# First x ahead of the vectors, first weights on ScalarE's queue, and of them only the first channel tile's columns at the beginning

## The chip, the core and the metric

The kernel runs on one core of one Trainium2 chip. The metric is the device time of one execution in microseconds (us), and lower is better. A profile of one execution was taken by the hardware profiler; its times, and all the rows below, are in us from the start of the span that the profile covers unless ns is written.

## What is computed

The reference is one layer of an encoder that works on 1024 frames of 1024 channels in float32. Cut to what matters here:

```python
h = rms_norm(x, norm1_g)
u = h @ w_in                                   # 1024 x 3072
u_conv, q, k, v, g = jnp.split(u, split_at, axis=-1)
a_out = conv_group(u_conv, ...)                # a * sigmoid(gate), causal conv of 31 taps, LayerNorm, silu
b_out = retention_group(q, k, v, g, ...)       # rotary, chunked retention, per-head RMSNorm, silu gate
x = x + concatenate([a_out, b_out]) @ w_out
h = rms_norm(x, norm2_g)
x = x + square(relu(h @ w_ff1)) @ w_ff2
return rms_norm(x, final_g)
```

The change touches only the beginning: the loads for `x`, for the first columns of `w_in` (those of `u_conv`), and the matmuls that use them.

## The kernel before

Every float32 operand of a large matmul is split in two parts, high and low: ScalarE writes a rounded copy (`split_row`, L116, for weights; `split_col`, L252, for columns of x, with the norm's gain as scale) and VectorE writes the rest (L117, L253). `mm3` (L149 to L151) multiplies high by high, high by low and low by high into one PSUM accumulator.

The program begins with `u_conv`. The x columns come as eight tiles `xc[i][h]` (i: a quarter of the 1024 channels, two rows of 128 each; h: a half of the frames), the weights as four tiles `raws[i]` of 128 x 2 x 512 (512 KB). A `raws[i]` holds four blocks of 128 columns: value and gate columns of channel tile j = 0, then those of channel tile j = 1. The loop at L326 goes through i; for each it splits `xc[i][0]`, `raws[i]` and `xc[i][1]` and issues the matmuls of channel tile 0 (`glu_proj(w, 0, ...)`), which use only the first 256 columns. The second 256 columns are used for the first time at L342, in `glu_proj(w, 1, ...)`.

Behind the loop come, in the code's order: the load of `dec`, then `stats(t)` for eight token blocks (load of 128 rows of x as `xt`, the sum of squares by ScalarE at L165, two small GpSimd operations), then `n2d` (L339), which writes 1024 single floats from `vec` to memory, 4 KB in all. Then TensorE does channel tile 1 for the first half of the frames (L342), and `pb` (L352): eight small matmuls of the matrix of ones with `diag` tiles that GpSimd builds from the norms (L351). ScalarE copies each half of `pb` out as `row` (L354). Then `trg` is loaded, `glu_gate(first)` runs, and `chunk_w(0)` loads and splits the next weights (`load_raw`, L112, then `split_row` on whole tiles); the remaining matmuls of channel tile 1 follow (second half of the frames).

What sets the order: TensorE, ScalarE and VectorE follow the code inside the `manual_schedule` block at L319; everywhere else, and for all transfers that SyncE issues, a scheduler arranges the instructions by their expected times, subject to the dependences. Each engine then carries out its own list strictly in that order, and one that waits holds up what stands behind it. All loads here are issued by SyncE (SPq in the rows). The weights' raw tiles come from the pool `rawp`, which has two buffers:

```python
rawp = pool("rawp", 2)
cp = pool("cp", 7)
```

so `raws[2]` takes the buffer of one of the first two tiles once that one has been split for the last time, and the transfer waits for this. The accumulators lie in two pools of four PSUM banks, `ps` and `pr`; `pb`'s two tiles and the accumulators of channel tile 1 take banks of `pr`, so the matmuls of channel tile 1's second half need the banks that `row` frees. Before the first real matmul TensorE does eleven matmuls of ones (L323), two passes each.

Of the kernel before, what the change touches and what calls it, by code (L numbers as in the profile page):

```python
# [8 lines left out]
F32 = mybir.dt.float32  # L9
F32R = mybir.dt.float32r  # L10
BF16 = mybir.dt.bfloat16
AF = mybir.ActivationFunctionType
ALU = mybir.AluOpType
PSUM = bass.MemoryType.PSUM

P = 128
D = 1024
S = 1024
CW = 512
# [6 lines left out]
ND = D // P  # L26
# [15 lines left out]
def hybrid_layer_kernel(  # L42
# [14 lines left out]
    nc = tc.nc  # L57
# [4 lines left out]
    rawp = pool("rawp", 2)  # L62
# [29 lines left out]
    cols = {}  # L92
# [19 lines left out]
        nc.sync.dma_start(raw, src)  # L112
        return raw

    def split_row(raw, w, i):
        nc.scalar.activation(w[:, 0, i], raw[:, i], AF.Copy)  # L116
        nc.vector.tensor_tensor(w[:, 1, i], raw[:, i], w[:, 0, i].bitcast(F32), ALU.subtract)  # L117

    def split(raw, scales):

        w = wp.tile([P, 2] + list(raw.shape[1:]), F32R, tag="w", name="w")
        for i in range(raw.shape[1]) if scales else [slice(None)]:
            if scales is None:
                split_row(raw, w, i)
            else:
                nc.scalar.activation(w[:, 0, i], raw[:, i], AF.Copy, scale=scales[i])
                nc.vector.scalar_tensor_tensor(
                    w[:, 1, i], raw[:, i], scales[i], w[:, 0, i].bitcast(F32), ALU.mult, ALU.subtract
                )
        return w  # L130
# [79 lines left out]
    def chunk_w(c):  # L210
        return [load_split(w_in[c, i], None) for i in range(ND // 2)]
# [32 lines left out]
    def split_cols(raw, dp, h):  # L244

        for i in range(2):
            split_col(raw, dp, h, i)

    def split_col(raw, dp, h, i):
        d = 2 * dp + i  # L250
        hi, lo = hT.half(d, 0, h), hT.half(d, 1, h)
        nc.scalar.activation(hi, raw[:, i], AF.Copy, scale=col("n1", d))  # L252
        nc.vector.scalar_tensor_tensor(lo, raw[:, i], col("n1", d), hi.bitcast(F32), ALU.mult, ALU.subtract)  # L253
# [16 lines left out]
    def glu_accs(j):  # L270
        return [[bank(j) for _ in range(2)] for _ in range(2)]

    def glu_proj(w, j, accs, d, h):

        for q in range(2):
            lo = (2 * j + q) * P
            mm3(
                accs[q][h],
                w[d // 2][:, 0, d % 2, lo : lo + P],
                w[d // 2][:, 1, d % 2, lo : lo + P],  # L280
                hT.half(d, 0, h),
                hT.half(d, 1, h),
                d == 0,
                d == ND - 1,
            )
# [18 lines left out]
    for h in range(2):  # L304
        hT.new(h)
    xc = [[cp.tile([P, 2, HALF], F32, tag="c", name="xcol") for _ in range(2)] for _ in range(ND // 2)]
    nc.sync.dma_start(vec, vecs)
    raws = [rawp.tile([P, 2, CW], F32, tag="raw", name="raw") for _ in range(ND // 2)]
    for i in range(2):
        nc.sync.dma_start(xc[0][0][:, i], x_cols[0, 0][:, i])  # L310
        nc.sync.dma_start(raws[0][:, i], w_in[1, 0][:, i])
    nc.sync.dma_start(xc[0][1], x_cols[0, 1])
    for i in range(1, ND // 2):
        nc.sync.dma_start(xc[i][0], x_cols[i, 0])
        nc.sync.dma_start(raws[i], w_in[1, i])
        nc.sync.dma_start(xc[i][1], x_cols[i, 1])
    w = []
    accs = glu_accs(0)
    with tc.manual_schedule(engines=ordered):  # L319

        idle = pr.tile([P, 4, P], F32, tag="r", name="idle")
        for i in range(WARM):
            nc.tensor.matmul(idle[:, i % 4], lhsT=ones, rhs=ones, start=True, stop=True)  # L323
        warm = tiny.tile([P, 1], F32, tag="ss1", name="warm")
        nc.scalar.activation(warm, mhalf[:, 0:1], AF.Square)
        for i in range(ND // 2):  # L326
            w.append(wp.tile([P, 2, 2, CW], F32R, tag="w", name="w"))
            for k in range(2):
                split_col(xc[i][0], i, 0, k)
                split_row(raws[i], w[i], k)  # L330
            split_cols(xc[i][1], i, 1)
            for h in range(2):
                for d in (2 * i, 2 * i + 1):
                    glu_proj(w, 0, accs, d, h)
# [39 lines left out]
    for g in range(NG):  # L374
        if g == NG - 1:
            w = chunk_w(2)
# [39 lines left out]
    w = wk  # L416
# [191 lines left out]
    i = 0  # L608
# [468 lines left out]
```

## Time and profile before

| what | value |
|---|---|
| median of 3 runs | 1037.97 us (1037.92 to 1038.72) |
| the profiled execution's own time | 1039.08 us |
| its span (first to last instruction) | 1037.1 us |
| mean granted TensorE clock in the span | 0.998 |
| TensorE busy | 1022.5 us, 99% |
| VectorE busy | 801.1 us, 77% |
| ScalarE busy | 380.9 us, 37% |
| GpSimd busy | 137.3 us, 13% |

The span is shorter than the execution's own time by 2.0 us, which lie before the first and behind the last instruction. A row of the timeline gives the start, the duration, the engine, the line in the code, what is written and read, how many instructions are merged in it, and in brackets how long the engine stood idle before and what released it. The rows of SPq are issues of transfers; the bytes land later.

### The profile page before, as it was taken

Reading aid. Unit: us, or ns where it says so; the run is one execution under the profiler, and the core shown is the slowest. Engines: PE = TensorE matmul, PEld = TensorE weight load, DVE = VectorE, ACT = ScalarE, POOL = GpSimd, SP = SyncE. Lnnn points to the kernel's source line nnn. Section 1 sums busy time; section 2 is a strip of 40 time slices with the busy share of each in tenths; the row PEclk is TensorE's granted clock in tenths of the full one; section 3 lists DMA queues with packets and bytes.
Section 4 is the critical chain, followed back from the end, with each engine's and each line's share of the span. In section 5 each row is a group of like instructions: output and inputs, shape, how many; then the busy total and the mean of one; then the engine's idle time right before and its main releaser. Section 6 shows DMA issues by size and latency. Waiting matters only on the chain.

```text
span 1037.1 us, 12617 instructions
## 1 busy us (share of the span) xinstructions
PE 1022.5 (99%) x4726; PEld 848.1 (82%) x4726; DVE 801.1 (77%) x981; ACT 380.9 (37%) x596; POOL 137.3 (13%) x253
## 2 busy tenths in 40 slices
PE   9999999999999999999999999999999999999997
PEld 7788888898888888878888888887888888888885
DVE  6297787998797659987777767766998778778765
ACT  7521121044531465543232333233443433433442
POOL 0410110012200233112121211211100000000013
PEclk9999999999999999999999999999999999999999
DMA  9722021102042047665363443548565355255214
GB/s 356 150 77 73 8 82 41 41 21 83 1 153 92 21 161 265 207 218 190 136 206 129 162 163 122 182 164 303 177 209 194 102 183 168 96 188 177 89 54 162
DMA packets 52876, 145.38 MB, mean 140 GB/s; under 512 B 6864, under 2 KB 16208, under 8 KB 52816
## 3 DMA queue, kind: packets, MB, share of 16 engines
q1 hardware_dynamic: 38000, 107.35, 31.5%
q0 software_dynamic: 10592, 35.14, 8.7%
q10 hardware_dynamic: 4224, 2.10, 0.7%
q8 instruction: 37, 0.61, 0.2%
q14 instruction: 23, 0.19, 0.1%
HBM read 103.14 MB, written 41.42 MB: 139 GB/s over the span
## 4 chain that ended last, share of the span: by engine, by line
PE 53%; DVE 3%; DMA 2%; issue 1%; ACT 0%; SPq 0%; POOLq 0%; POOL 0%; ACTq 0%; DVEq 0%
PE acc L149 9%; PE acc L150 9%; PE acc L151 9%; PE pa L151 5%; PE pa L149 5%; PE pa L150 5%; PE pb L151 4%; PE pb L150 4%; PE pb L149 4%; DMA w2raw<-in_w_dram 2%; DVE w L203 1%; DVE blk L949 0%; DVE hid L758 0%; ACT w L200 0%; DVE w1l L203 0%
## 5 line engine op out<-in xcount | busy, mean ns | idle before, releaser
L149 PE MATMUL acc<-w 128*128 128x512 f32 x448 | 174.7, 390 | 1.1 <-DVE hid L758 0.8
L151 PE MATMUL acc<-w 128*128 128x512 f32 x448 | 174.3, 389 | 0.0
L150 PE MATMUL acc<-w 128*128 128x512 f32 x448 | 174.3, 389 | 0.0
L395 DVE SCALAR_TENSOR_TENSOR y<-glu,vec,y 128x1024 f32<-128x1024 f32 x120 | 153.7, 1289 | 2.0
L149 PEld LDWEIGHTS acc<-w 128*128 128x128 f32 x448 | 84.1, 188 | 20.0 <-issue 1.4
L149 PE MATMUL acc<-w,cols 128*128 128x512 f32 x256 | 100.1, 391 | 0.0
L150 PE MATMUL acc<-w,cols 128*128 128x512 f32 x256 | 99.8, 390 | 0.0
L151 PE MATMUL acc<-w,cols 128*128 128x512 f32 x256 | 99.8, 390 | 0.0
L151 PEld LDWEIGHTS acc<-w 128*128 128x128 f32 x448 | 84.1, 188 | 17.5
L150 PEld LDWEIGHTS acc<-w 128*128 128x128 f32 x448 | 84.1, 188 | 17.2
L200 ACT ACTIVATE w<-xr 128x1024 fp32r<-128x1024 f32 x56 | 59.2, 1058 | 98.8 <-PE acc L151 44.4
L203 DVE TENSOR_TENSOR w<-xr,w 128x1024 fp32r<-128x1024 f32 x56 | 68.3, 1220 | 28.2 <-ACT w L200 27.8
L949 DVE TENSOR_TENSOR blk<-acc,blk 128x512 f32<-128x512 f32 (+1 forms) x113 | 72.8, 680 | 17.0 <-PE acc L151 17.0
L149 PE MATMUL pa<-h,w1h 128*128 128x512 f32 x192 | 74.8, 393 | 0.5 <-ACT w1h L200 0.5
L151 PE MATMUL pa<-h,w1l 128*128 128x512 f32 x192 | 75.0, 392 | 0.1
L149 PE MATMUL pb<-h,w1h 128*128 128x512 f32 x192 | 74.8, 389 | 0.0
L151 PE MATMUL pb<-h,w1l 128*128 128x512 f32 x192 | 74.7, 389 | 0.0
L150 PE MATMUL pb<-h,w1h 128*128 128x512 f32 x192 | 74.7, 389 | 0.0
L203 DVE TENSOR_TENSOR w1l<-t,w1h 128x1024 fp32r<-128x1024 f32 x32 | 39.1, 1223 | 43.4 <-PE pb L150 40.1
L116 ACT ACTIVATE w<-raw 128x1024 fp32r<-128x1024 f32 (+1 forms) x32 | 30.5, 954 | 87.8 <-PE acc L151 70.3
L151 PEld LDWEIGHTS acc<-w,cols 128*128 128x128 f32 x256 | 48.1, 188 | 10.0
L149 PEld LDWEIGHTS acc<-w,cols 128*128 128x128 f32 x256 | 48.1, 188 | 9.8
(194 smaller groups left out, 2003.8 us busy)
## 6 DMA issues: line engine op xcount, KB each, us to landing
w1raw<-in_w_dram SPq DMA_DIRECT2D x32, 512.0 KB, 4.7
w2raw<-in_w_dram SPq DMA_DIRECT2D x32, 512.0 KB, 4.5
raw<-in_w_in_dram SPq DMA_DIRECT2D x23, 512.0 KB, 3.3
xt<-in_x_dram SPq DMA_DIRECT2D x8, 512.0 KB, 7.9
raw<-in_w_out_dram SPq DMA_DIRECT2D x8, 512.0 KB, 3.2
xr<-in_x_dram SPq DMA_DIRECT2D x16, 256.0 KB, 3.0
kept<-blk POOLq DMA_DIRECT2D x8, 512.0 KB, 3.3
blk<-kept SPq DMA_DIRECT2D x8, 512.0 KB, 4.7
```

The source lines that it names most:

```text
L116: nc.scalar.activation(w[:, 0, i], raw[:, i], AF.Copy)
L149: nc.tensor.matmul(acc, lhsT=lh, rhs=rh, start=first, stop=False, **kw)
L150: nc.tensor.matmul(acc, lhsT=lh, rhs=rl, start=False, stop=False, **kw)
L151: pe_log.append(nc.tensor.matmul(acc, lhsT=ll, rhs=rh, start=False, stop=last, **kw))
L200: act = nc.scalar.activation(hi, src, AF.Copy)
L203: nc.vector.tensor_tensor(lo, src, hi.bitcast(F32), ALU.subtract)
L395: nc.vector.scalar_tensor_tensor(y, glu[c][:, k : k + S], tap(k), y, ALU.mult, ALU.add)
L949: return nc.vector.tensor_tensor(t, acc[lane][r][:, lo:hi], t, ALU.add)
```

## The change

The load of the first half of `xc[0][0]` goes in front of that of the vectors `vec`. The first row of `raws[0]` is issued by ScalarE, as its first instruction, the second row by SyncE; both bring only the first 256 columns. The other 256 columns of both rows (`then`) are loaded by one transfer that stands in the code behind those of i = 2, and are split behind the loop's last splits.

```diff
-    def split_row(raw, w, i):
-        nc.scalar.activation(w[:, 0, i], raw[:, i], AF.Copy)
-        nc.vector.tensor_tensor(w[:, 1, i], raw[:, i], w[:, 0, i].bitcast(F32), ALU.subtract)
+    def split_row(raw, w, i, cols=slice(None)):
+        nc.scalar.activation(w[:, 0, i, cols], raw[:, i, cols], AF.Copy)
+        nc.vector.tensor_tensor(w[:, 1, i, cols], raw[:, i, cols], w[:, 0, i, cols].bitcast(F32), ALU.subtract)
...
+    raws = [rawp.tile([P, 2, CW], F32, tag="raw", name="raw") for _ in range(ND // 2)]
+    now, then = slice(0, 2 * P), slice(2 * P, CW)
+    nc.scalar.dma_start(raws[0][:, 0, now], w_in[1, 0][:, 0, now])
+    nc.sync.dma_start(xc[0][0][:, 0], x_cols[0, 0][:, 0])
     nc.sync.dma_start(vec, vecs)
-    raws = [rawp.tile([P, 2, CW], F32, tag="raw", name="raw") for _ in range(ND // 2)]
-    for i in range(2):
-        nc.sync.dma_start(xc[0][0][:, i], x_cols[0, 0][:, i])
-        nc.sync.dma_start(raws[0][:, i], w_in[1, 0][:, i])
+    nc.sync.dma_start(raws[0][:, 1, now], w_in[1, 0][:, 1, now])
+    nc.sync.dma_start(xc[0][0][:, 1], x_cols[0, 0][:, 1])
     nc.sync.dma_start(xc[0][1], x_cols[0, 1])
     for i in range(1, ND // 2):
         nc.sync.dma_start(xc[i][0], x_cols[i, 0])
         nc.sync.dma_start(raws[i], w_in[1, i])
         nc.sync.dma_start(xc[i][1], x_cols[i, 1])
+        if i == 2:
+            nc.sync.dma_start(raws[0][:, :, then], w_in[1, 0][:, :, then])
...
-                split_row(raws[i], w[i], k)
+                split_row(raws[i], w[i], k, now if i == 0 else slice(None))
             split_cols(xc[i][1], i, 1)
+            if i == ND // 2 - 1:
+                split_row(raws[0], w[0], slice(None), then)
```

SyncE's list, from the first transfer of i = 1 on. The number behind a name is that of the tile: before, `raws[0]` to `raws[3]` are raw_126 to raw_129, now they are raw_125 to raw_128; xcol_117 to xcol_124 are `xc[0][0]` to `xc[3][1]`. Before:

```order
L314 DMA xcol_119<-in_x_cols_dram 128x1024
L315 DMA raw_127<-in_w_in_dram 128x1024
L316 DMA xcol_120<-in_x_cols_dram 128x1024
L314 DMA xcol_121<-in_x_cols_dram 128x1024
L315 DMA raw_128<-in_w_in_dram 128x1024
L316 DMA xcol_122<-in_x_cols_dram 128x1024
L314 DMA xcol_123<-in_x_cols_dram 128x1024
L315 DMA raw_129<-in_w_in_dram 128x1024
L316 DMA xcol_124<-in_x_cols_dram 128x1024
L335 DMA dec_100<-in_decay_dram 128x576
L259 DMA xt_314<-in_x_dram 128x1024
```

There each `raws[i]` stood between the two x tiles of its i, and `raws[3]` ahead of `dec`. SyncE's list in the same place now:

```order
L316 DMA xcol_119<-in_x_cols_dram 128x1024
L317 DMA raw_126<-in_w_in_dram 128x1024
L318 DMA xcol_120<-in_x_cols_dram 128x1024
L316 DMA xcol_121<-in_x_cols_dram 128x1024
L318 DMA xcol_122<-in_x_cols_dram 128x1024
L317 DMA raw_127<-in_w_in_dram 128x1024
L320 DMA raw_125<-in_w_in_dram 128x2x256
L316 DMA xcol_123<-in_x_cols_dram 128x1024
L318 DMA xcol_124<-in_x_cols_dram 128x1024
L341 DMA dec_100<-in_decay_dram 128x576
L317 DMA raw_128<-in_w_in_dram 128x1024
L259 DMA xt_317<-in_x_dram 128x1024
```

The transfer of `raws[2]` (raw_127) stands behind both x tiles of i = 2, and that of `raws[3]` (raw_128) behind `dec`, the last place before the eight `xt`. `raws[0]` keeps its buffer until `then` has been split, so the other three tiles follow each other in the one buffer that is left: in the built program raw_127's transfer waits for VectorE's second split of raw_126, and raw_128's for the second split of raw_127. Before, raw_128 waited for the second split of raw_126, and raw_129 for that of raw_127: the tile two places ahead, now it is the tile just ahead.

ScalarE's list around the two copies `row`, from the last sum of squares (`trash`) to the second split of the next weights. Before, the first weight tile of `chunk_w(0)` is raw_483, split into w_485:

```order
L165 ACTIVATE trash_379,ss_380<-xt_375 128x1024
L354 ACTIVATE row_449<-pb_436 128x512
L116 ACTIVATE w_485<-raw_483 128x1024
L354 ACTIVATE row_464<-pb_451 128x512
L296 ACT_TABLE_LOAD
L296 ACTIVATE sg_471<-zg_469 128x512
L116 ACTIVATE w_490<-raw_488 128x1024
```

There the first `row` stood ahead of that split. In ScalarE's list now, in the same place, the tile is raw_486, split into w_488:

```order
L165 ACTIVATE trash_382,ss_383<-xt_378 128x1024
L116 ACTIVATE w_488<-raw_486 128x1024
L360 ACTIVATE row_452<-pb_439 128x512
L360 ACTIVATE row_467<-pb_454 128x512
L296 ACT_TABLE_LOAD
L296 ACTIVATE sg_474<-zg_472 128x512
L296 ACTIVATE sg_481<-zg_479 128x512
```

The split of the next weights stood between the two copies and now stands ahead of both. In TensorE's list, five matmuls of the second half stood between the wait for the first `row` and the wait for the second; now four stand there. Beyond the first glu gates (some 60 us into the program) the lists of all engines are the same as before.

## Rows read from the trace of the kernel before

**Rows 1.** The page's first part: busy time, share of the span, instructions.

```profile
PE 1022.5 (99%) x4726; PEld 848.1 (82%) x4726; DVE 801.1 (77%) x981; ACT 380.9 (37%) x596; POOL 137.3 (13%) x253
```

**Rows 2.** TensorE's waits: who waited for whom, us in total, times, longest.

```profile
PE acc L149 <- ACT row L354: 1.9, 1, 1.9
```

**Rows 3.** Timeline of TensorE: start, us, engine, line, out<-in, [idle before <-releaser].

```profile
1.04 4.70 PE L323 MATMUL idle<-ones 128*128 128x128 f32 x22 [1.04 <-DVE ones L82]
6.16 0.50 PE L149 MATMUL acc<-cols,w 128*128 128x512 f32 x1 [0.42 <-ACT w L116]
...
39.27 1.95 PE L352 MATMUL pb<-diag,ones 128*128 128x128 f32 x16
41.08 0.50 PE L149 MATMUL acc<-cols,w 128*128 128x512 f32 x1
...
44.42 0.50 PE L149 MATMUL acc<-cols,w 128*128 128x512 f32 x1 [1.94 <-ACT row L354]
```

**Rows 4.** Timeline of ScalarE from the sums of squares to the second row.

```profile
22.68 1.06 ACT L165 ACTIVATE trash<-xt 128x1024 bf16<-128x1024 f32 x1 [0.25 <-DMA xt<-in_x_dram]
...
31.63 1.06 ACT L165 ACTIVATE trash<-xt 128x1024 bf16<-128x1024 f32 x1 [0.15 <-DMA xt<-in_x_dram]
...
40.42 0.60 ACT L354 ACTIVATE row<-pb 128x512 f32<-128x512 f32 x1 [7.64 <-PE pb L352]
42.82 1.06 ACT L116 ACTIVATE w<-raw 128x1024 fp32r<-128x1024 f32 x1 [1.80 <-DMA raw<-in_w_in_dram]
43.79 0.58 ACT L354 ACTIVATE row<-pb 128x512 f32<-128x512 f32 x1
```

**Rows 5.** Timeline of SyncE's issues: raws[2], and n2d.

```profile
8.41 0.33 SPq L315 DMA_DIRECT2D raw<-in_w_in_dram  x1
...
24.28 0.43 SPq L339 DMA_DIRECT2D n2d<-vec  x1
```

**Rows 6.** Issues at 8.41, 24.28 and 45.16: count, KB, us to landing.

```profile
raw<-in_w_in_dram SPq DMA_DIRECT2D x1, 512.0 KB, 6.9
...
n2d<-vec SPq DMA_DIRECT2D x1, 4.0 KB, 16.5
...
raw<-in_w_in_dram SPq DMA_DIRECT2D x1, 512.0 KB, 3.4
```

**Rows 7.** Timelines of ScalarE and VectorE: splits of raws[1], raws[2], raws[3].

```profile
11.61 0.63 ACT L116 ACTIVATE w<-raw 128x512 fp32r<-128x512 f32 x1 [0.56 <-DMA raw<-in_w_in_dram]
...
19.44 0.63 ACT L116 ACTIVATE w<-raw 128x512 fp32r<-128x512 f32 x1 [0.51 <-DMA raw<-in_w_in_dram]
...
13.56 0.69 DVE L117 TENSOR_TENSOR w<-raw,w 128x512 fp32r<-128x512 f32 x1
...
17.41 0.68 DVE L117 TENSOR_TENSOR w<-raw,w 128x512 fp32r<-128x512 f32 x1
```

**Rows 8.** Transfer rate, 40 slices each, of 0 to 30 and of 28 to 46.

```profile
GB/s 0 0 108 146 191 300 322 306 317 377 426 404 415 426 404 432 421 421 421 415 421 421 426 388 407 400 436 418 426 415 399 410 421 426 421 415 415 421 426 293
...
GB/s 437 410 419 285 259 347 310 56 64 36 27 9 73 27 9 46 18 9 46 55 73 82 36 27 55 109 91 91 264 419 346 282 218 173 36 0 0 0 0 0
```

**Rows 9.** Timeline of GpSimd: the last four diag tiles.

```profile
35.51 2.35 POOL L351 TENSOR_SCALAR diag<-ident,r 128x128 f32<-128x128 f32 x4
```

**Rows 10.** Stretches: us, busy PE, PEld, DVE, ACT, POOL (count), clock, DMA share, GB/s.

```profile
42.40:44.40 2.00, 0.08 (x1) 0.00 (x0) 0.49 (x1) 1.56 (x3) 0.00 (x0) 1.00 0.24 96
...
1022.00:1029.90 7.90, 7.90 (x35) 6.20 (x34) 5.83 (x9) 2.17 (x6) 3.00 (x6) 1.00 0.48 187
1029.90:1032.60 2.70, 0.01 (x1) 0.00 (x0) 2.08 (x4) 0.91 (x4) 1.23 (x4) 1.00 0.47 182
1032.60:1037.10 4.50, 0.00 (x0) 0.00 (x0) 0.75 (x1) 0.72 (x1) 0.10 (x1) 0.50 0.52 201
```

**Rows 11.** Stretches of the matmuls of ones: us, TensorE busy (count), clock, DMA, GB/s.

```profile
1.04:4.20 3.16, 3.16 (x15) 1.00 0.68 148
...
5.20:5.75 0.55, 0.54 (x5) 1.00 0.91 305
```

## The prediction

> **What bounds the kernel now.** I read the busy times first: TensorE is busy for 1022.5 us of the span [rows 1], so time is won or lost only where TensorE stands idle. Then TensorE's waits: the longest is 1.9 us on `row`, ScalarE's copy of `pb` [rows 2]. Then TensorE's timeline. The matmuls of ones run from 1.04 to 5.74, the first real matmul starts at 6.16 after 0.42 us of idling for a weight split, and the 144 matmuls before `pb` then need 33.1 us, up to 39.27 [rows 3]. At the pitch of a stretch without gaps, 7.90 us for 35 matmuls or 0.226 us each [rows 10], 144 of them take 32.6 us, so another 0.5 us of small gaps lies in there. After `pb`, five matmuls run from 41.08, and TensorE waits until 44.42 for the second `row` [rows 3].
>
> Why is that `row` late? On ScalarE the first copy runs at 40.42, the split of the next weights waits for its transfer until 42.82, and only then comes the second copy, done at 44.37 [rows 4]. That transfer is late because of `n2d`: issued at 24.28, its 4 KB land 16.5 us later, at 40.8 [rows 5, 6]. The rates say the same: the transfers run gapless at some 420 GB/s from 7.5 to 29.4 us, then comes a hole of some 9 us with tens of GB/s, and the rate is back only at 40.6 [rows 8]. So the chain that ends last in this stretch is: transfers saturated up to the last `xt` (used at 31.63 [rows 4]), then `n2d`, then `trg` and the weight tile at 42.8, then ScalarE, then TensorE. Everything TensorE does before 41 us has slack against it.
>
> **The start.** The first split now waits for a 256 KB x tile in front of the 78 KB of vectors, and the weights are not behind either on SyncE. TensorE can't start its real matmuls before the matmuls of ones end, at 5.74, so at most 0.42 us is gained here, and at most another 0.5 us from the small gaps. ScalarE's issue in front of its table load costs nothing: some 0.4 us of ScalarE, which then idles for the first x tile anyway. All of this gain arrives ahead of the `row` wait, which doesn't depend on TensorE, so it is worth 0 in the sum (and 0.9 if that wait went away).
>
> **The weight tiles.** `raws[0]` holds its buffer until the end of the loop, so `raws[2]` is issued only when `raws[1]` has been split, and `raws[3]` when `raws[2]` has been. I follow these times.
> (1) `raws[1]` landed at 11.6 [rows 7]. Now 256 KB fewer lie ahead of it; at the 300 to 420 GB/s of these slices [rows 8] that is 0.6 to 0.9 us: 10.8.
> (2) From its landing to the end of VectorE's second split were 2.65 us (11.6 to 13.56 + 0.69) [rows 7], so `raws[2]` is issued at 13.45; before, it was issued at 8.41 and landed at 15.3 [rows 5, 6].
> (3) By then the x tiles ahead of it are nearly through (3.8 us for three tiles of 512 KB, 14.6). A transfer issued to idle queues takes 3.4 us [rows 6], one behind a full queue 6.9; I take 3.4, since the queue runs dry: landing at 16.8. The transfers stand empty for some 1.5 us meanwhile.
> (4) From that landing to the second split's end were 2.8 us (15.3 to 17.41 + 0.68) [rows 7]: `raws[3]` is issued at 19.65 and lands 3.3 to 3.4 us later, at 23.0. Before, it landed at 19.4 [rows 7]. Behind `dec` the queue is nearly empty once more.
> TensorE, reaching `raws[2]` and `raws[3]` at about 17 and 23 us, loses some 0.5 us at each and comes to `pb` at 40.3 rather than 39.27: still inside the slack.
>
> **The sums of squares and `n2d`.** All eight `xt` are now issued behind `raws[3]`: nine transfers of 512 KB, at 420 GB/s 1.25 us each. Of the 3.4 us of a transfer issued to idle queues, 1.25 are its bytes, so I let bytes flow from some 1.5 us after the issue, 21.1; nine tiles end at about 32.4, where the full rate ended at 29.4 and the rest trickled to 31 before [rows 8]. By bytes that is 2.4 us later, counted to the middle of that end; by landings (the old 12.2 us from `raws[3]` to the last `xt` less the 1.95 of an x tile and `dec`, which now go ahead) 1.5. I take 2.2. ScalarE splits `then` (1.06 us, as for a tile of 1024 columns [rows 4]) ahead of the sums: they start at 27.1 rather than 22.68 and end at 36.9; GpSimd's last `diag` came 5.2 us after the last sum (31.63 + 1.06 to 35.51 + 2.35 [rows 4, 9]), so it comes at 42.1. So TensorE finishes `pb` at 42.2, later than before by about 1 us, and still ahead of the weight tile. Bytes and order of `n2d` are unchanged, so I move its hole as a whole: the weight tile lands at 42.8 + 2.2 = 45.0.
>
> **Behind it.** ScalarE now splits that tile before either `row`. The first copy ends 1.6 us after the landing (0.97 to the start, 0.60 for it [rows 4]), at 46.6. Before, TensorE was released at 44.42 and had already done five of these matmuls (5 x 0.226 = 1.13 us); now it is released at 46.6 with none of them done, and the second copy comes while the next four run. The loss is 2.2 + 1.13 = **3.3 us**; without the delay of the transfers it would be 1.1. The bounds: 0.8 (`raws[1]` as early as 10.2, the transfers never empty) to 4.7 (each of the two tiles 0.6 us later).
>
> **The clock.** TensorE now stands idle from 42.2 to 46.6, 4.4 us. In the trace it stays at 2.4 GHz (granted clock 1.00) through the 2 us of 42.4 to 44.4, but after the last matmul at 1029.9 it is 1.00 for 2.7 us and then 0.50, that is 1.2 GHz [rows 10]. The new gap is longer than both, so I expect the clock to fall in it. What that costs: at the beginning fifteen matmuls of ones take 3.16 us and, from 5.2 on, five take 0.54 [rows 11], so about half the speed for the first 4.2 us; a stretch like that after the gap costs half of it, 2.1 us, a short one 0.4. I take 1.5, nearer to the row. The Trainium skill, in "TensorE: Matmul & The Clock Gate", section "HAM oscillation — how this bites in real kernels", says that a long wait for a transfer throttles the engine again and that the next burst starts cold. By that rule the time is the one forecast here, and without it 1.5 us less; the trace agrees at its end and shows no such gap in the middle. The sum: 3.3 + 1.5 = **4.8 us**.
>
> **The rivals.** (A) As forecast: late transfers, the split ahead of both `row`, and the clock falls. (B) The same, but the clock stays at 1.00, as in the 2 us gaps: +3.3. (C) The transfers close up, because the queue hides the one-buffer chain after all: only the order on ScalarE costs, +1.1. For it speaks that the total of bytes is the same; against it the two issues that wait for a split. (D) Not slower at all: `n2d`'s hole is shorter. It was issued 7 us before the transfers ahead of it ended; now it is issued at 28.6, some 4 us before. If its slow writes pass while less is queued with them, so that the weight tile lands before 42.8 - 1.13 = 41.7, the five matmuls are repaid. With the shift of 2.2 that takes a hole of under 6 us in place of the 9.4 from 31.2 to 40.6 [rows 8]; at 4.5 us the time is 1.6 us less than before. Nothing in the change touches those 1024 writes, so I give this little.
>
> **How the numbers follow.** Added to the profiled execution's own 1039.08 the forecast is 1043.9; the median of the runs lies 1.1 lower, and I predict for it: 1037.97 + 4.8 = 1042.8 us. Chances: A 0.58; B 0.24 (1041.3); C 0.12 (1039.1); D 0.06 (1036.4). A runs from 1041.0 (delay 1.5, clock 0.4) to 1044.8, B from 1039.9 to 1042.7. The range of 1040.2 to 1044.6 leaves out C, D and the outer ends of A and B. About 0.2%, or 2.1 us, is what a measurement can tell from no change: slower takes A and nearly all of B, 0.80; the same takes C and a corner of B, 0.14; faster D, 0.06.
>
> **What would show it.** In the new profile: the first real matmul at about 5.75 with no wait ahead of it (the gain that is there and isn't kept); SyncE's issues of `raws[2]` at 13.5 and of `raws[3]` at 19.6, with a dip in the rate at 14 to 15 and 20 to 21; the first sum of squares at about 27; `n2d` issued at 28.6; the split of the next weights at about 45, both `row` behind it; TensorE waiting some 4.4 us for `row` at about 46.6, and a stretch of granted clock 0.50 behind. Wrong would be: `raws[3]` landing before 21, a weight tile landing before 43.5, a wait for `row` under 2.5 us, or a new wait of TensorE after 60 us.

## The result, and the profile after

The changed kernel takes 1044.06 us (median of 6 runs, 1042.78 to 1047.96) against 1038.03 us of the kernel before (6 runs, 1036.62 to 1039.78): a ratio of 1.0056, 95% interval 1.0043 to 1.0068, or 5.8 us more. The forecast was 4.8 more, 1042.8 us, with 1044.6 as the range's upper end. The profiled execution took 1044.4 us, its span 1042.5, 5.4 more than before. All times below are from the start of a span.

TensorE's waits in the changed kernel (who waited for whom, us in total, times, longest) answer to [rows 2]:

```profile
PE acc L149 <- ACT row L360: 3.2, 1, 3.2
...
PE acc L149 <- ACT w L116: 1.3, 1, 1.3
```

The wait for `row` grew from 1.9 to 3.2 us, and a wait for the split of `raws[3]` is new. TensorE's timeline in the changed kernel, beside [rows 3] (start, duration, engine, line, out<-in, idle before and its releaser):

```profile
5.81 0.79 PE L149 MATMUL acc<-cols,w 128*128 128x512 f32 x1
...
25.27 0.50 PE L149 MATMUL acc<-cols,w 128*128 128x512 f32 x1 [1.31 <-ACT w L116]
...
42.04 1.95 PE L358 MATMUL pb<-diag,ones 128*128 128x128 f32 x16
47.17 0.54 PE L149 MATMUL acc<-cols,w 128*128 128x512 f32 x1 [3.18 <-ACT row L360]
47.51 0.63 PE L150 MATMUL acc<-cols,w 128*128 128x512 f32 x1
47.94 0.63 PE L151 MATMUL acc<-cols,w 128*128 128x512 f32 x1
...
50.92 0.40 PE L149 MATMUL acc<-cols,w 128*128 128x512 f32 x1
51.15 0.39 PE L150 MATMUL acc<-cols,w 128*128 128x512 f32 x1
...
59.77 0.39 PE L149 MATMUL acc<-w,cols 128*128 128x512 f32 x1
```

The first real matmul starts 0.35 us earlier than before, without a wait. `pb` is reached at 42.04 rather than 39.27, and TensorE goes on at 47.17 rather than 44.42. From there the matmuls follow at 0.43 us, from 50.9 on at 0.23. The last row is the first matmul of `proj_group`, the first one that uses the weights of `chunk_w(0)`; in the kernel before it starts at 54.34. That is a good mark: 59.77 - 54.34 = 5.43, the whole difference of these two spans. Between these two traces, all of the loss arises in the first 60 us.

ScalarE's timeline in the changed kernel, beside [rows 4, 7]: the first splits of `raws[1]`, `raws[2]`, `raws[3]`, the first and the last sum of squares, the next weights' split and the first `row`:

```profile
11.19 0.63 ACT L116 ACTIVATE w<-raw 128x512 fp32r<-128x512 f32 x1 [0.53 <-DMA raw<-in_w_in_dram]
...
17.21 0.63 ACT L116 ACTIVATE w<-raw 128x512 fp32r<-128x512 f32 x1 [2.41 <-DMA raw<-in_w_in_dram]
...
24.59 0.63 ACT L116 ACTIVATE w<-raw 128x512 fp32r<-128x512 f32 x1 [2.53 <-DMA raw<-in_w_in_dram]
...
28.01 1.04 ACT L165 ACTIVATE trash<-xt 128x1024 bf16<-128x1024 f32 x1
...
35.35 1.06 ACT L165 ACTIVATE trash<-xt 128x1024 bf16<-128x1024 f32 x1
...
45.57 1.06 ACT L116 ACTIVATE w<-raw 128x1024 fp32r<-128x1024 f32 x1 [9.08 <-DMA raw<-in_w_in_dram]
46.54 0.58 ACT L360 ACTIVATE row<-pb 128x512 f32<-128x512 f32 x1
```

SyncE's issues of `raws[2]`, `raws[3]` and `n2d` in the changed kernel, beside [rows 5]:

```profile
13.86 0.33 SPq L317 DMA_DIRECT2D raw<-in_w_in_dram  x1
...
19.87 0.33 SPq L317 DMA_DIRECT2D raw<-in_w_in_dram  x1
...
29.54 0.43 SPq L345 DMA_DIRECT2D n2d<-vec  x1
```

And the clock: stretches of the changed kernel behind `pb`, with the columns of [rows 10] (us; busy time of PE, PEld, DVE, ACT, POOL with counts; granted clock; DMA share; GB/s):

```profile
43.99:47.17 3.18, 0.00 (x1) 0.00 (x1) 0.51 (x1) 1.60 (x3) 0.00 (x0) 1.00 0.23 94
47.17:50.90 3.73, 3.73 (x9) 2.93 (x10) 1.92 (x3) 2.76 (x4) 0.33 (x1) 0.54 0.45 141
50.90:59.77 8.87, 8.87 (x41) 7.32 (x39) 6.69 (x8) 5.03 (x6) 4.36 (x3) 1.00 0.18 62
```

After a gap of 3.18 us TensorE works at 1.2 GHz (granted clock 0.54 as the mean of this stretch) for most of 3.7 us, and then at 2.4 GHz. The Trainium skill says in "TensorE: Matmul & The Clock Gate", section "HAM oscillation — how this bites in real kernels", that a long wait for a transfer throttles the engine again and the next burst starts cold. The rows above agree: the wait is 3.18 us at 1.00, the stretch behind it 0.54. One of the experiments below shows that a shorter wait can do it too.

### The profile page after: what moved, and what is told of

The parts are those of the page before. It is cut to its first block, busy times and chain, and to the rows that moved or that the text cites. A ratio compares the mean times of both kernels' runs of the same rounds, so it can differ in the third digit from the quotient of the medians.

```text
span 1042.5 us, 12616 instructions
## 1 busy us (share of the span) xinstructions
PE 1025.1 (98%) x4726; PEld 849.6 (81%) x4726; DVE 800.3 (77%) x982; ACT 379.9 (36%) x597; POOL 138.1 (13%) x253
## 4 chain that ended last, share of the span: by engine, by line
PE 55%; DVE 1%; DMA 1%; ACT 0%; issue 0%; POOLq 0%; POOL 0%; ACTq 0%; DVEq 0%
PE acc L149 10%; PE acc L151 10%; PE acc L150 10%; PE pa L151 5%; PE pa L149 5%; PE pa L150 5%; PE pb L150 4%; PE pb L151 4%; PE pb L149 4%; DMA w2raw<-in_w_dram 1%; DVE hid L764 0%; DVE w1l L203 0%; DVE part L802 0%; DVE h L203 0%; ACT w1h L200 0%
## 5 line engine op out<-in xcount | busy, mean ns | idle before, releaser
L116 ACT ACTIVATE w<-raw 128x1024 fp32r<-128x1024 f32 (+2 forms) x33 | 30.7, 930 | 103.1 <-PE acc L151 70.5
L117 DVE TENSOR_TENSOR w<-raw,w 128x1024 fp32r<-128x1024 f32 (+2 forms) x33 | 36.1, 1092 | 28.5 <-ACT w L116 28.3
L149 PEld LDWEIGHTS acc<-w,cols 128*128 128x128 f32 x256 | 48.1, 188 | 9.9
```

The source lines that it names most:

```text
L116: nc.scalar.activation(w[:, 0, i, cols], raw[:, i, cols], AF.Copy)
L117: nc.vector.tensor_tensor(w[:, 1, i, cols], raw[:, i, cols], w[:, 0, i, cols].bitcast(F32), ALU.subtract)
L149: nc.tensor.matmul(acc, lhsT=lh, rhs=rh, start=first, stop=False, **kw)
```

## The experiments

The theory has three terms: the next weight tile lands later, because `raws[2]` and `raws[3]` follow each other through one buffer and push everything behind them; ScalarE splits that tile ahead of both `row`, so the five matmuls are no longer done while it is awaited; and the clock falls in the gap. Against it stand: one of the terms is the whole loss, the clock costs nothing, or the loss lies elsewhere. Each kernel below was compared with the kernel before on the same chip. The 26 to 31 runs of the kernel before spread over 6.6 to 8.0 us there, and the intervals of the ratios are 0.9 to 2.0 us to either side, so the traces carry the finer readings; differences in us below follow from the ratios.

**The first part alone**, on the kernel before:

```diff
-    nc.sync.dma_start(vec, vecs)
...
-    for i in range(2):
-        nc.sync.dma_start(xc[0][0][:, i], x_cols[0, 0][:, i])
-        nc.sync.dma_start(raws[0][:, i], w_in[1, 0][:, i])
+    nc.scalar.dma_start(raws[0][:, 0], w_in[1, 0][:, 0])
+    nc.sync.dma_start(xc[0][0][:, 0], x_cols[0, 0][:, 0])
+    nc.sync.dma_start(vec, vecs)
+    nc.sync.dma_start(raws[0][:, 1], w_in[1, 0][:, 1])
+    nc.sync.dma_start(xc[0][0][:, 1], x_cols[0, 0][:, 1])
```

> The kernel before with the first part alone: x ahead of the vectors, the first weight row issued by ScalarE, whole tiles as before. The tiles of weights keep their places, so the next weight tile should land at 42.8 us as before. But the scheduler puts that tile's split ahead of both copies row here too. Theory (order on ScalarE, then the clock): the first row is done at 44.4, TensorE idles from 40.2 to 44.4 and resumes without the five matmuls: +1.1 us, and +1.6 more where the clock falls to 1.2 GHz, +2.7 in all. Rival 1 (only the late transfers cost, as the part of the sum for the start with its 0 said): 0. Rival 2 (the start is gained in full): -0.5 to -0.9.

Measured: 1.0006 (0.9993 to 1.0020), +0.6 us with -0.7 to +2.1: within the noise, and below the 2.7 expected. ScalarE's timeline of this run:

```profile
41.75 1.06 ACT L116 ACTIVATE w<-raw 128x1024 fp32r<-128x1024 f32 x1 [9.17 <-DMA raw<-in_w_in_dram]
42.71 1.07 ACT L355 ACTIVATE row<-pb 128x512 f32<-128x512 f32 x2
```

and TensorE's:

```profile
6.66 0.50 PE L149 MATMUL acc<-cols,w 128*128 128x512 f32 x1 [0.98 <-ACT w L116]
...
43.34 0.50 PE L149 MATMUL acc<-cols,w 128*128 128x512 f32 x1 [1.86 <-ACT row L355]
```

The split stands ahead of both `row`, as in the change, but the tile came 1.07 us earlier than in the trace of before, which pays for the five matmuls (1.13; why the tile came earlier is not shown). The mark is at 54.34, as before. Two steps of the expectation fell: `pb` was reached at 39.5, not 38.4, so the gap was 1.86 us, and the clock didn't fall in it. Nor is there a gain at the start here: with whole weight rows the first real matmul waits 0.98 us.

**A buffer of its own** for the later columns, in the changed kernel:

```diff
+    rest = sp.tile([P, 2, CW - 2 * P], F32, tag="s", name="rest")
...
-            nc.sync.dma_start(raws[0][:, :, then], w_in[1, 0][:, :, then])
+            nc.sync.dma_start(rest, w_in[1, 0][:, :, then])
...
-                split_row(raws[0], w[0], slice(None), then)
+                nc.scalar.activation(w[0][:, 0, :, then], rest, AF.Copy)
...
```

> The changed kernel, but the columns that come later (then) are loaded into a buffer of their own, so that raws[0] frees its buffer early: raws[2] and raws[3] are no longer chained through one buffer. The scheduler then also puts row, split, row in the old order. Theory (buffer chain): raws[3] lands by 20.5 us rather than 24.6, the first sum of squares starts at 23.5 to 24 rather than 28.0, the next weight tile lands at 42.8 to 43.2, TensorE is released at 44.4: 0 against the kernel before, up to +1.6 if the clock falls in a gap of some 3 us. Rival 1 (the smaller, split transfers themselves are slow, whatever the buffer): the tile still lands at 45 or later and the time stays at +3 or more. Rival 2 (the loss lies behind 60 us): +5 to +6 as with the change.

Measured: 0.9998 (0.9985 to 1.0011). The chain through one buffer is gone, and with it the loss. ScalarE's timeline (`raws[3]`, the first sum, then row and split):

```profile
19.48 0.63 ACT L116 ACTIVATE w<-raw 128x512 fp32r<-128x512 f32 x1 [0.52 <-DMA raw<-in_w_in_dram]
...
22.90 1.04 ACT L165 ACTIVATE trash<-xt 128x1024 bf16<-128x1024 f32 x1
...
41.52 0.60 ACT L362 ACTIVATE row<-pb 128x512 f32<-128x512 f32 x1 [7.80 <-PE pb L360]
42.01 1.05 ACT L116 ACTIVATE w<-raw 128x1024 fp32r<-128x1024 f32 x1
```

`raws[3]` is split at 19.48 (before 19.44, changed 24.59), the sums start at 22.90, and the tile is there when the first `row` has been copied: its split follows without a wait. The split transfers by themselves cost nothing that shows. Since the scheduler also restores the old order on ScalarE, this run takes away all three terms at once.

This trace shows one thing more. Its span is 1039.1 us, 2.0 more than before, although its mark comes 0.6 us earlier. At 250 us TensorE's `pstate` matmuls wait for ScalarE's `state`, as they do in all fourteen traces, here for 1.82 us, and behind that wait its clock is low (stretches, columns as above):

```profile
248.62:250.44 1.82, 0.00 (x0) 0.00 (x0) 1.82 (x3) 1.68 (x3) 0.00 (x0) 1.00 0.02 5
250.44:254.20 3.76, 3.76 (x20) 3.66 (x21) 3.76 (x4) 1.52 (x3) 0.00 (x0) 0.62 0.60 170
```

In the other thirteen traces the same wait lasts 1.58 to 1.93 us, and the clock stays at 1.00 there.

**Both rows first**: the changed kernel with its late transfers, and the next weights' split held behind both copies (the helper `hold` adds such an order between two instructions of one engine):

```diff
-        nc.scalar.activation(w[:, 0, i, cols], raw[:, i, cols], AF.Copy)
+        act = nc.scalar.activation(w[:, 0, i, cols], raw[:, i, cols], AF.Copy)
+        if behind:
+            hold(act, behind[-1])
...
-        nc.scalar.activation(row, pb.rearrange("p i t -> p (i t)"), AF.Copy)
+        behind.append(nc.scalar.activation(row, pb.rearrange("p i t -> p (i t)"), AF.Copy))
```

> The changed kernel with all its transfers as they are, but the next weights' split is held behind both copies row on ScalarE. Theory (the row copies hang on a transfer that they don't need): the tile still lands at 45.5, but TensorE, done with pb at 44.0, resumes at 44.0 to 44.2, the clock stays at 2.4 GHz; five matmuls later than before by 0.7: +0.7 us against the kernel before, -5 against the change. Rival 1 (the late transfers cost by themselves, in the sums of squares or in the next weights): +3 to +4. Rival 2 (TensorE waits next for the split of the next weights at some 53 us): +2.

Measured: 1.0002 (0.9989 to 1.0014). TensorE's timeline here (lines are four higher):

```profile
41.98 1.95 PE L362 MATMUL pb<-diag,ones 128*128 128x128 f32 x16
43.78 0.50 PE L153 MATMUL acc<-cols,w 128*128 128x512 f32 x1
```

No wait stands behind `pb`. `raws[3]` is as late as with the change (split at 24.58) and TensorE reaches `pb` 2.7 us later than before, but that is paid, all but 0.43 us at the mark, by the 1.94 us of waiting that go away. So the late transfers cost, as far as the interval of 1.3 us can tell, through one thing only: copies that stand behind a split which waits for them.

**The old order with the late transfers**: first row, split, second row, as before. The load of `trg` and the first tile of `chunk_w(0)` are written between the two rows, and the split is held behind the first:

```diff
+        if h == 0:
+            nc.sync.dma_start(trg, trig)
+            behind.append(copy)
+            wv = [load_split(w_in[0, 0], None)]
+            behind.clear()
...
-    wv = chunk_w(0)
+    wv += [load_split(w_in[0, i], None) for i in range(1, ND // 2)]
```

> The changed kernel with its late transfers, and on ScalarE the kernel before's order: first row, the next weights' split, second row. This is the cell that is missing between the runs so far (late transfers with both rows first: +0.2; early transfers with row, split, row: -0.2; early transfers with the split ahead of both: +0.6; late transfers with the split ahead of both: +5.8). The tile lands at 44.1 to 47 in the four traces with late transfers. Theory (late tile, order and clock are three terms): TensorE does five matmuls behind pb, then waits for the second row for some 1 to 2.5 us; released at 45.7 to 48.6 with five done: +1.3 to +4.2, middle +2.7; the clock stays at 1.00. Rival 1 (the order is the whole loss): +0.2 to +0.7. Rival 2 (the order is worth nothing): +5 to +6.

Measured: 1.0039 (1.0022 to 1.0055), +4.1 us with 2.3 to 5.7; the middle is above the 2.7 expected, and rival 1 is out. By the time alone rival 2, from +5, is not. The trace settles it better. ScalarE's timeline:

```profile
46.27 1.06 ACT L118 ACTIVATE w<-raw 128x1024 fp32r<-128x1024 f32 x1 [1.38 <-DMA raw<-in_w_in_dram]
47.23 0.58 ACT L364 ACTIVATE row<-pb 128x512 f32<-128x512 f32 x1
```

and TensorE's:

```profile
47.86 0.50 PE L153 MATMUL acc<-cols,w 128*128 128x512 f32 x1 [1.74 <-ACT row L364]
```

The tile is 3.45 us later than in [rows 4], TensorE's release 3.44 later than in [rows 3]. Four matmuls stand between `pb` and this wait in the trace, five before, so this is the first term by itself but for one matmul.

**n2d behind the two weight tiles**, in the changed kernel: its two lines are moved down, to the loop over `wk`.

> The changed kernel with n2d issued behind the first two of the next weight tiles instead of ahead of trg and of these; ScalarE's list is as with the change, the split ahead of both rows. Theory (the tile is late because it stands behind n2d's slow 1024 writes): the last xt lands at 35 as with the change, trg and the two tiles at 36 to 38, the split is done by 38.5, ahead of pb, TensorE waits for row under 0.5 us, the clock stays: +0.2 to +0.7 against the kernel before, -5 against the change. Rival 1 (the tile is late because the transfers before it are late): it lands above 42 all the same, +4 to +6. Rival 2 (n2d, behind them now, delays the third and fourth weight tile, and TensorE waits for these at 55 to 60): +2 to +4.

Measured: 1.0012 (0.9999 to 1.0024). ScalarE's timeline:

```profile
38.30 1.06 ACT L116 ACTIVATE w<-raw 128x1024 fp32r<-128x1024 f32 x1 [1.27 <-DMA raw<-in_w_in_dram]
43.77 0.60 ACT L358 ACTIVATE row<-pb 128x512 f32<-128x512 f32 x1 [4.41 <-PE pb L356]
```

The split is still ahead of both rows, but it starts 7.3 us earlier, at 38.30 rather than 45.57, and is done 4.4 us before the first row is copied. The tile was late because it stood behind `n2d`, and the order on ScalarE does no harm once it doesn't. Of the 1.2 us that are left the trace has 1.1 at the mark: TensorE waits 1.8 us for `raws[3]` there.

**Matmuls that fill the gap**: the changed kernel, and TensorE repeats the last matmul of `pb`, nine times in one run and twelve in the next:

```diff
+        for _ in range(9 * h):
+            nc.tensor.matmul(pb[:, 3], lhsT=ones, rhs=diag, start=True, stop=True)
```

> The changed kernel, and TensorE repeats the last matmul of pb nine times (the same values are written again), so that it is busy for 2.2 us of the 3.2 us in which it waits for row; everything else stays in place, row is released at the same 47.2. Theory (the clock is a term of its own): the granted clock stays at 1.00 behind the wait, the matmuls there keep 0.227 us, and the time is 1.6 us below the change: +4.0 against the kernel before. Rival (the low clock behind the wait hides beside another wait): no difference from the change, +5.8. Second rival (the clock falls all the same): +5.8 with a stretch of 0.50.

Measured with nine: 1.0041 (1.0023 to 1.0058). It decided nothing on the term's size: the tile was split at 47.0 in that trace, 3.0 us of idling were left, and the clock fell behind them:

```profile
45.57:48.59 3.02, 0.01 (x1) 0.00 (x0) 0.50 (x1) 1.59 (x3) 0.00 (x0) 1.00 0.22 88
48.59:52.24 3.65, 3.65 (x9) 2.89 (x10) 1.92 (x3) 2.67 (x4) 0.24 (x1) 0.53 0.45 139
```

> As the run with nine repeats of pb's last matmul, but with twelve (2.9 us): with nine, 3.0 us of idling were left because the tile landed at 47.0, and the clock fell. Now 0.3 to 1.7 us are left, by where the tile lands (45.5 to 47). Theory (the clock is a term of its own, 1.6 us): granted clock 1.00 behind the wait, matmuls at a pitch of 0.227 us there, +4.0 against the kernel before and 1.6 below the change. Rival 1 (the low clock hides beside another wait): +5.6 as the change. Rival 2 (the clock falls with the length of the wait for row, whatever TensorE does in it): a stretch of 0.50 again, +5.6.

Measured with twelve: 1.0052 (1.0037 to 1.0067). Stretch of its trace from TensorE's release to the first matmul of `proj_group`:

```profile
45.76:56.74 10.98, 10.98 (x48) 9.12 (x49) 6.98 (x10) 6.60 (x8) 4.62 (x3) 1.00 0.33 98
```

Here 0.34 us of idling were left, the clock stays at 1.00, and the same matmuls that took 47.17 to 59.77, 12.60 us, in the change take 10.98. So the clock is a term of 1.6 us in the traces, and no later wait swallows it. The median doesn't show it: +5.4 us, interval 3.8 to 7.0, holds both the 4.0 and the 5.6 of the expectations. The profiled run was the fastest of the six, and its tile was split at 44.16; how late it came in the others isn't recorded. By time this stays open.

**The change once more**, on the chip of the runs with row, split, row and with the wait of fixed length:

> The changed kernel once more, on the chip of these runs, for comparison with the fillers: +5 to +6 against the kernel before. Theory: the weight tile lands at 44 to 47 as n2d's hole varies, and where TensorE's gap is over 3 us the clock falls for some 3.4 us behind it. Rival (the first trace was an exception): the tile at 43 or earlier and no fall.

Measured: 1.0060 (1.0040 to 1.0079). Stretches behind `pb`:

```profile
43.61:48.12 4.51, 0.00 (x1) 0.00 (x1) 0.51 (x1) 1.60 (x3) 0.00 (x0) 0.78 0.43 149
48.12:52.94 4.82, 4.82 (x11) 3.79 (x12) 2.02 (x4) 2.87 (x4) 1.42 (x2) 0.50 0.36 109
52.94:61.38 8.44, 8.44 (x39) 6.95 (x37) 7.21 (x9) 4.84 (x5) 3.13 (x2) 1.00 0.28 74
```

The tile was split at 46.52, the gap is 4.51 us, and the clock was already low at its end; 4.8 us of work are slow, and release to mark takes 13.26. In these six runs the time goes with the mean clock: 1043.7 us at 0.999, 1045.4 and 1045.6 at 0.997 and 0.996, 1046.3 to 1047.2 at 0.993 and 0.994. A later tile lengthens the gap and the time as well, so this doesn't separate the two. It does suggest that the clock doesn't fall in every run of the change: the fastest of its first six runs, too, has the highest mean clock (1042.8 us at 0.998).

**A wait of fixed length**, without `n2d` in it, was meant to measure the clock's term by time, with and without the repeated matmuls:

```diff
-        nc.scalar.activation(row, pb.rearrange("p i t -> p (i t)"), AF.Copy)
+        for _ in range(8 - 7 * h):
+            nc.scalar.activation(row, pb.rearrange("p i t -> p (i t)"), AF.Copy)
```

> A wait for row of a fixed length, that doesn't hang on n2d: n2d is issued late (as in the run where it stands behind the two weight tiles), and ScalarE makes the first copy row eight times in a row (0.53 us each), so that TensorE, done with pb at 44.4, is released at about 48.1, after 3.6 us. Theory (a gap of over 3 us lets the clock fall): a stretch of granted clock 0.50 of about 3.4 us behind it, matmuls at 0.43 us there; against the kernel before 1.2 for n2d late, 3.6 for the wait, 1.6 for the clock: +6.4. Rival (the clock doesn't count): +4.8.

> The same fixed wait, and TensorE repeats the last matmul of pb twelve times in it (2.9 us), so that 0.7 us of idling are left; row is released at the same 48.1. Theory (the clock is a term of its own, 1.6 us): granted clock 1.00 throughout, matmuls at 0.227 us behind the wait: +4.8 against the kernel before, 1.6 below the run without repeats. Rival (what the low clock costs hides beside a later wait): the same time as without repeats.

Measured: 1.0016 (1.0002 to 1.0030) and 1.0048 (1.0033 to 1.0063). The pair failed: without the repeats TensorE was released after only 1.6 us, at 45.15, four copies after the first one's start, so the second row's copy seems to stand among the eight of the first, and the clock didn't fall. With them it was released at 47.88, also at full clock: the repeats filled 2.84 us of its wait, and 1.44 us of idling were left. Release to mark took 11.13 and 10.99 us, once more the length at 2.4 GHz.

**Both rows first in the kernel before:**

> The kernel before, and only the next weights' split is held behind both copies row on ScalarE. Theory (the wait for row is the one thing that holds TensorE there, and nothing is late next): pb ends at 41.1, TensorE goes on without a wait; the 1.94 us go away, of which 1 to 1.9 in the median, since the wait varies with n2d: -1.0 to -1.9 against the kernel before. Rival (the next weights, split later, hold TensorE at some 53 us, or the glu gates hold the accumulators): 0 to +0.5.

Measured: 1037.71 us, 0.9985 (0.9974 to 0.9995), 1.6 us less with 0.5 to 2.7. TensorE's timeline:

```profile
39.11 1.95 PE L356 MATMUL pb<-diag,ones 128*128 128x128 f32 x16
40.91 0.50 PE L153 MATMUL acc<-cols,w 128*128 128x512 f32 x1
```

The wait is gone and nothing takes its place. **The changed kernel with its own buffer and both rows first:**

> The changed kernel with both cures: the later columns in a buffer of their own, and the next weights' split behind both copies row. Theory (with the wait for row gone, an earlier start is kept): first real matmul at 5.8 rather than 6.16, pb reached at 39.0 to 40.4, no wait behind it: -1.0 to -2.3 against the kernel before. Rival 1 (the transfers of the first tiles bound TensorE up to pb, as 0.8 us of waiting for the second tile's split showed with the own buffer alone; the start gain is lost there): no better than the kernel before with the rows first, or up to 0.8 worse: -0.2 to -1.9. Rival 2 (the next weights become the bound at some 53 us): 0.

Measured: 1037.85 us, 0.9989 (0.9980 to 0.9998). TensorE's timeline:

```profile
5.82 0.80 PE L153 MATMUL acc<-cols,w 128*128 128x512 f32 x1
...
8.31 0.50 PE L153 MATMUL acc<-cols,w 128*128 128x512 f32 x1 [0.31 <-ACT w L118]
...
40.24 1.95 PE L364 MATMUL pb<-diag,ones 128*128 128x128 f32 x16
```

It starts 0.2 us earlier than the run above, waits 0.31 us at the second matmul group of the loop, and reaches `pb` 1.1 us later: rival 1. With the cover of the `row` wait taken away, the earlier start still brings nothing. Both versions are clear of the kernel before and of the change, and neither is clear of the other.

## The sum, kernel by kernel

From the traces: when the next weights' tile is split, how many of the five matmuls are done at TensorE's release, the release, the mark (first matmul of `proj_group`), its shift against before, and the sum of the terms: the tile's delay against 42.82, 0.226 us for each of the five that isn't done (1.13 for all), and what release to mark takes beyond the 10.98 to 11.00 us that it takes at full clock with none done.

| kernel | tile split | of five | release | mark | shift | terms |
|---|---|---|---|---|---|---|
| before | 42.82 | 5 | 44.42 | 54.34 | | |
| the change | 45.57 | 0 | 47.17 | 59.77 | +5.43 | 2.75 + 1.13 + 1.6 = 5.5 |
| the change again | 46.52 | 0 | 48.12 | 61.38 | +7.04 | 3.70 + 1.13 + 2.3 = 7.1 |
| nine repeats | 47.00 | 0 | 48.59 | 61.24 | +6.90 | 4.18 + 1.13 + 1.7 = 7.0 |
| twelve repeats | 44.16 | 0 | 45.76 | 56.74 | +2.40 | 1.34 + 1.13 = 2.5 |
| row, split, row | 46.27 | 4 | 47.86 | 57.97 | +3.63 | 3.45 + 0.23 = 3.7 |
| first part alone | 41.75 | 0 | 43.34 | 54.34 | 0.00 | -1.07 + 1.13 = 0.1 |

Six traces agree with the three terms to within 0.1 us. The clock's term is read off the same trace, so its size is not tested by this. What is tested: TensorE is released 1.6 us after the split's start in all seven, and the shift less delay and clock is 1.05 to 1.07 us in all five with none done. Where no `row` waits for that tile, the terms are gone and TensorE's own progress decides (own buffer -0.6, both rows first +0.4, both rows first in the kernel before -2.4).

The table ends at the mark. Behind it, up to the span's end, the fourteen traces differ from before by another -0.6 to +2.6 us: +2.6 with the own buffer, +2.0 with nine repeats, +1.4 with twelve, 0.0 for the change. Apart from the own buffer's low clock at 250 us, what makes these was not looked into.

## Why the prediction was right, and where its sizes were off

**The start** came as said: no wait, first real matmul at 5.81 (5.75), worth nothing in the sum. The other traces showed that even this small gain isn't sure: the wait was 0.98 us with the first part alone, and with the change's own loads 0.50 us in the run with nine repeats and 0.61 with both rows first.

**The one-buffer chain** was right in its order: `raws[2]` issued at 13.86 (13.45) and split at 17.21 (16.8), `raws[3]` issued at 19.87 (19.65). Step (1) was 0.4 us off: `raws[1]` is split at 11.19, and the 256 KB that no longer lie ahead of it brought no more than that. **The term that was mis-sized is step (4)**: `raws[3]` was to land 3.3 to 3.4 us after its issue, "behind `dec` the queue is nearly empty once more". It came after 4.7 us, at 24.59 rather than 23.0. What had been issued just before was still under way, as the transfers' list of the changed kernel shows (issues of 13 to 33 us, then the one at 19.87 by itself: count, KB, us to landing):

```profile
xcol<-in_x_cols_dram SPq DMA_DIRECT2D x2, 512.0 KB, 6.7
...
dec<-in_decay_dram SPq DMA_DIRECT2D x1, 288.0 KB, 7.3
raw<-in_w_in_dram SPq DMA_DIRECT2D x1, 256.0 KB, 4.3
n2d<-vec SPq DMA_DIRECT2D x1, 4.0 KB, 13.4
...
raw<-in_w_in_dram SPq DMA_DIRECT2D x1, 512.0 KB, 4.7
```

`dec`, issued at 16.04, landed 7.3 us later, at 23.3: the transfers that the wait for `raws[2]` had held up filled the queue for `raws[3]`. They also moved more slowly than the 420 GB/s of the prediction, at 224 to 295 GB/s from 16 to 20 us; why is not shown. So the sums start at 28.01 (27.1), the last at 35.35, `n2d` is issued at 29.54 (28.6), and the tile is split at 45.57 (45.0): 2.75 us late rather than 2.2. The other traces with the chain say 44.16 to 47.00, mean of five 45.9; those without it in which the split waits for the tile say 42.82, 41.75 and 42.56, mean 42.4. By these means the term is nearer to 3.5 than to 2.2, with 1.4 us of spread to either side. `n2d`'s hole did move as a whole: from the last sum's start to the tile's split are 10.2 us in the change and 11.2 before.

TensorE's stalls on the way were not 0.5 us each: no wait shows at `raws[2]`, and the one at `raws[3]` is 1.31 us. With smaller gaps it came to `pb` at 42.04 rather than 40.3, 0.3 us behind the last `diag` (41.77, predicted 42.1), and `pb` ended at 43.99 rather than 42.2. It cost nothing, as argued, since the tile came later still.

**The order on ScalarE** was to cost 1.13 us and cost 1.06: that is what is left of the shifts when the tile's delay and the clock are taken off, and all but one matmul of it is absent with row, split, row.

**The clock** fell, after a gap of 3.18 us rather than 4.4, and cost 1.6 us (1.5 predicted; 2.3 in the second trace). That the size came out so close is partly luck. The prediction took it between 0.4 and 2.1 from the slow matmuls of ones, for which [rows 11] show a granted clock of 1.00, so these rows do not show that their half speed was the clock's; and its gap came out 1.2 us shorter. The length of a gap alone doesn't settle whether the clock falls, as the waits at 250 us show.

Rival B, in which the clock stays, is out by both traces of the change, rival C by the tile's landing, rival D since the hole was 1 us shorter, not the 3.4 that it needed. Of the 1.0 us between the 4.8 predicted and the 5.8 measured the profiled trace gives 0.55 to the tile's delay and 0.1 to the clock; the rest lies within the interval, and in the mean of the traces the delay is larger still.

**The bounds** of the loss without the clock don't fit together: 0.8 is used as a delay (B's lower end, 1039.9, is 0.8 + 1.13 above the kernel before), while 4.7 is a loss; two tiles 0.6 us later each would give 2.2 + 1.2 + 1.13 = 4.5. The forecast itself doesn't hang on them.

## What to carry to other kernels

A small copy that frees an accumulator must not stand behind work that waits for a transfer: one order between two instructions of ScalarE took back the loss (+0.2 us was left, within the noise), and it made the kernel before 1.6 us faster. Loading a part of a tile late keeps the whole tile's buffer until that part has been used; with two buffers in the pool that turned a pair into a chain, and a buffer of its own for the late part undid it. Before an earlier start is bought, look for the next wait whose end doesn't hang on it.

## What the hardware showed beyond that

`n2d`'s 4 KB take 13.0 to 16.5 us to land in these traces, and they hold off the others: with `n2d` moved behind it, the weight tile was split 7.3 us earlier. Stretches of the changed kernel ahead of its writes and in them (columns as above):

```profile
31.00:34.00 3.00, 3.00 (x15) 2.49 (x14) 0.00 (x0) 3.00 (x7) 2.11 (x7) 1.00 1.03 384
...
36.00:42.50 6.50, 6.50 (x33) 5.44 (x32) 0.00 (x0) 0.50 (x2) 5.70 (x11) 1.00 0.81 79
```

The rate falls from 384 to 79 GB/s while the engines' busy share only goes from 1.03 to 0.81. The length of this stretch varies: the weight tile came anywhere between 44.2 and 47.0 us in five traces with the same transfers. Much of the spread of the runs may come from this, with the clock on top where it falls; that was not shown run by run. What speaks for it: where a `row` waits for that tile in the trace, the runs' standard deviation is 1.0 to 2.2 us, and in the seven kernels where none does it is 0.4 to 1.2, least with the own buffer and both rows first, 0.4.

Behind `pb` the clock fell with the gaps of 3.02, 3.18 and 4.51 us, and with none of 1.94 us or less; but the own buffer's trace has it fall behind a wait of 1.82 us at 250 us, where waits of up to 1.93 us left it at 1.00 in the others. So a gap's length alone doesn't tell. It didn't fall at the gap's start: in the change it was still 1.00 all through the 3.18 us, and the slow stretch came behind the gap, when TensorE was at work again.
